# Delta heads of a hybrid decoder: the norm factors of the queries by Newton steps on GpSimd, where a logarithm on ScalarE stood

## The chip, the cores and the metric

The kernel runs on one core of a Trainium2 chip, in one launch. The metric is the device time of that launch in microseconds (us). A time quoted for a kernel is the median of its runs; a profile shows one more execution, which has a time of its own.

The engines are named as in the profile: PE is TensorE (matmuls), PEld its weight loads, DVE is VectorE, ACT is ScalarE, POOL is GpSimd, and SP issues most of the DMAs.

## The reference

Two decoder layers in a row, for 512 prompt tokens and 8 samples of 8 tokens, 576 tokens in all. Each layer has one wide input projection, three branches (a gated linear recurrence, differential attention, gated DeltaNet, 4 heads each), a merge, an output projection, and a gated MLP. Only the DeltaNet branch, the delta heads, matters here:

```python
def l2norm(x):
    return xf * lax.rsqrt(jnp.sum(xf * xf, axis=-1, keepdims=True) + EPS)
...
    q_g = l2norm(cq.reshape(b, L, GD_HEADS, GD_DK)) * (GD_DK ** -0.5)
    k_g = l2norm(ck.reshape(b, L, GD_HEADS, GD_DK))
...
    o_g, gd_s = gdn_chunked(q_g, k_g, v_g, beta, loga, gd_s0)
...
    o_c = (rmsnorm(o_g, w['gdn_norm']) * oz).reshape(b, L, -1).astype(x.dtype)
```

`gdn_chunked` is the gated delta rule, worked block-wise: `o` is linear in the query, and inside a block a unit lower-triangular system with one matrix per block is solved. cq, ck and cv come out of a causal convolution of width 4 and a SiLU.

## The kernel before, in words

**The matmul stream.** Almost all of PE's time goes to the dense projections, in float32 precision. A block of weights `raw` is split into a high part `wh` (a cast on ACT, L264) and a low part `wl` = raw - wh (a subtraction on DVE; `tt`, L197, is the helper that records all two-input tensor operations), and each of the products xh·wh, xl·wh and xh·wl is a matmul into `acc` (recorded at L190, as all matmuls and transposes are). The split parts lie in a pool of three buffers, so that ACT and DVE run about two blocks ahead of PE.

**The order.** `drive` writes the program: dense jobs one after the other, and between their groups of matmuls the steps of stages (a head is a stage) on three lanes. It keeps a model clock that counts the matmuls written so far; a stage says `yield 1.4` where its next matmul wants a result that is to take so long, and is taken up again when the model clock has moved on by that much. On top of it the Tile scheduler orders the instructions of each engine by its own estimate of costs. An engine runs its list strictly in that order.

**A delta head** (`gdn_head`, 4 heads in each of 2 layers) goes through these steps.

- `conv_silu` for the keys, then the sums of squares of the keys, `ss[:, 0]`, and `Ln` of them. From these come the scales `u2` and `w1`.
- `conv_silu` for the queries, and the first weights products (`r<-ckq` on PE).
- The inverse of the triangular matrices in blocks of 16: `cm` goes out by a DMA into `da` and comes back as `dtr` with another layout. A loop of 15 steps, two small DVE operations `dtr<-dtr` each, works out the inverse. It is copied (L858), goes out into `dt` and comes back as `ctt` by DMAs (L860 to L863). Eight DVE operations spread it into `TB`.
- Beside it, `conv_silu` for the values into `cv` (its tanh, `ct`, is L740; its last product on DVE is L742), and the block from L875 on: the queries are transposed and squared on ACT with the sums in `ss[:, 1]` (L880), and `cn`, the factor 1/(norm of the query · sqrt(128)) relative to that of the keys, is worked out of `ss` by a logarithm and an exponential (L881 to L886).
- The larger blocks of the inverse on PE: three rounds, the first of which begins with `r<-TB,ap`. Then the recurrence over four blocks, and the samples' part.
- `finish_gated` at the head's end calls `head_norm` (L491), the only reader of `cn`: it multiplies the mean squares of the output `ot` by `cn` twice, takes `rsqrt` (Newton's steps on DVE, in the kernel already for this), and multiplies the result by `cn`.

Other names in the rows: `XX` is work of the recurrent branch, that the scheduler places beside the delta heads; `thb` (L704) is the SiLU of the output gates; `P<-` on POOL (L1288) clears a tile of attention; `cb<-hg` (L726) copies convolution rows. `L1315` is attention's exponential.

ACT holds one table of functions at a time: a profile row `ACT_TABLE_LOAD` stands wherever the next function needs another one.

Of the kernel before, what the change touches and what calls it, by code (L numbers as in the profile page):

```python
# [11 lines left out]
F32 = mybir.dt.float32  # L12
F32R = mybir.dt.float32r
BF16 = mybir.dt.bfloat16
I32 = mybir.dt.int32
U8 = mybir.dt.uint8
AF = mybir.ActivationFunctionType
ALU = mybir.AluOpType
# [21 lines left out]
EPS = 1e-6  # L40
# [107 lines left out]
def kernel(ctx, tc, a, o, depth=DEPTH, dbg=None):  # L148
    nc = tc.nc
    V, S, G, PE = nc.vector, nc.scalar, nc.gpsimd, nc.tensor  # L150
# [7 lines left out]
    sm = pool('sm', bufs=3)  # L158
# [15 lines left out]
    def bc(ap, n):  # L174
        sh = list(ap.shape)
        return ap.rearrange('p (x o) -> p x o', o=1).to_broadcast([sh[0], sh[1], n])
# [19 lines left out]
    def tt(out, in0, in1, op, eng=None):  # L196
        (eng or V).tensor_tensor(out=out, in0=in0, in1=in1, op=op)  # L197
# [51 lines left out]
    b4e = cst.tile([128, 1], F32, name='b4e')  # L249
# [3 lines left out]
    def rsqrt(out, v, n):  # L253

        y, w = out, sm.tile([128, 20], F32, tag='rs_w', name='rs_w')[:, :n]
        V.tensor_scalar(out=y.bitcast(I32), in0=v.bitcast(I32), scalar1=1, scalar2=None, op0=ALU.logical_shift_right)
        V.tensor_scalar(out=y.bitcast(I32), in0=y.bitcast(I32), scalar1=-1, scalar2=0x5F3759DF, op0=ALU.mult, op1=ALU.add)
        for _ in range(3):
            tt(w, y, y, ALU.mult)
            V.scalar_tensor_tensor(out=w, in0=w, scalar=-0.5, in1=v, op0=ALU.mult, op1=ALU.mult)  # L260
            V.scalar_tensor_tensor(out=y, in0=w, scalar=1.5, in1=y, op0=ALU.add, op1=ALU.mult)

    def split(src, hi, lo):
        S.copy(hi, src)  # L264
        tt(lo, src, hi, ALU.subtract)
# [175 lines left out]
    def norm_stats(sa, rb, r):  # L441

        ps = rp()
        for j in range(5):
            mm(ps[:, j:j + 1], sa[:, 128 * j:128 * j + 128], ones[:, 0:1])
        ms = sm.tile([128, 5], F32, tag='ms', name='ms')
        V.memset(ms, 1.0)
        V.tensor_scalar(out=ms[:, 0:4], in0=ps[:, 0:4], scalar1=1.0 / D_MODEL, scalar2=EPS, op0=ALU.mult, op1=ALU.add)
        V.tensor_scalar(out=ms[:NS, 4:5], in0=ps[:NS, 4:5], scalar1=1.0 / D_MODEL, scalar2=EPS, op0=ALU.mult, op1=ALU.add)
        rsqrt(r, ms, 5)  # L450
        dg = gt.tile([128, T], F32, tag='th', name='dg')
        tt(dg[:, :SEQ].rearrange('p (j t) -> p j t', j=4), bc1(ident, 4), bc(r[:, 0:4], 128), ALU.mult)
        V.tensor_scalar(out=dg[:, SEQ:], in0=ident[:, :NS], scalar1=r[:, 4:5], scalar2=None, op0=ALU.mult)
        yield
        pb, pb2 = rp(), rp()
        mm(pb, ones, dg[:, :SEQ])
        mm(pb2[:, :NS], ones, dg[:, SEQ:])
        S.copy(rb[:, :SEQ], pb)
        S.copy(rb[:, SEQ:], pb2[:, :NS])
# [31 lines left out]
    def head_norm(ot, p, cn=None):  # L491

        sq = p.tile([128, 5, 128], F32, tag='hn', name='hn')
        ms = sm.tile([128, 5], F32, tag='ms', name='ms')
        for j in range(5):
            S.activation(sq[:, j], ot[:, j], AF.Square, accum_out=ms[:, j:j + 1])
        for _ in range(0 if cn is None else 2):
            tt(ms, ms, cn, ALU.mult)
        V.tensor_scalar(out=ms, in0=ms, scalar1=1.0 / 128, scalar2=EPS, op0=ALU.mult, op1=ALU.add)
        r = sm.tile([128, 5], F32, tag='ln_r', name='ln_r')  # L500
        rsqrt(r, ms, 5)
        if cn is not None:
            tt(r, r, cn, ALU.mult)
        tt(ot, ot, bc(r, 128), ALU.mult)
# [133 lines left out]
    for l in range(depth):  # L638
# [82 lines left out]
        def conv_silu(acc, ci, dst):  # L721

            P = cvp.tile([128, 604], F32, tag='cb', name='cb')
            Ps = P[:, 515:603].rearrange('p (b j) -> p b j', j=11)
            G.memset(P[:, 0:3], 0.0)
            G.tensor_copy(Ps[:, :, 0:3], hg[:, ci])  # L726
            tt(P[:, 3:3 + HALF], acc[:, 0], rb[:, 0:HALF], ALU.mult)
            tt(P[:, 3 + HALF:515], acc[:, 1, 0:224], rb[:, HALF:SEQ], ALU.mult)
            tt(Ps[:, :, 3:11], acc[:, 1, 224:288].rearrange('p (b j) -> p b j', j=8),
               rb[:, SEQ:].rearrange('p (b j) -> p b j', j=8), ALU.mult)  # L730
            G.tensor_copy(gco[:, ci, 0, :], P[:, 512:515])
            G.tensor_copy(gco[:, ci, 1:9, :], Ps[:, :, 8:11])
            A = cvp.tile([128, 604], F32, tag='ca', name='ca')
            w = F['gconv']
            S.activation(A[:, 0:600], P[:, 0:600], AF.Copy, scale=w[:, 4 * ci:4 * ci + 1])
            for j in range(1, 4):
                V.scalar_tensor_tensor(out=A[:, 0:600], in0=P[:, j:j + 600], scalar=w[:, 4 * ci + j:4 * ci + j + 1],  # L737
                                       in1=A[:, 0:600], op0=ALU.mult, op1=ALU.add)
            th = gt.tile([128, 604], F32, tag='th', name='ct')
            S.activation(th[:, 0:600], A[:, 0:600], AF.Tanh, scale=0.5)  # L740
            sv = lambda t: t[:, 515:603].rearrange('p (b j) -> p b j', j=11)[:, :, 0:8]
            V.scalar_tensor_tensor(out=dst[:, 0:SEQ], in0=th[:, 0:SEQ], scalar=1.0, in1=A[:, 0:SEQ], op0=ALU.add, op1=ALU.mult)  # L742
            V.scalar_tensor_tensor(out=dst[:, SEQ:].rearrange('p (b j) -> p b j', j=8), in0=sv(th), scalar=1.0, in1=sv(A),
                                   op0=ALU.add, op1=ALU.mult)

        def gdn_head(h, p):
# [15 lines left out]
            ss = sm.tile([128, 2, 5], F32, tag='ss', name='ss')  # L762
# [8 lines left out]
            for j in range(5):  # L771
                n = 128 if j < 4 else NS
# [51 lines left out]

            pc = parts()
            conv_silu(acc, h, ckq[:, 1, 0:T])
            ex = sm.tile([128, 2, 5], F32, tag='ex', name='ex')
            V.tensor_copy(ex[:, 0], u2)
            tt(ex[:, 1], w1, GL[:, :, h], ALU.add)
            S.activation(ex, ex, AF.Exp)  # L830
            nk = sm.tile([128, 5], F32, tag='nk', name='nk')
            V.tensor_scalar(out=nk, in0=ex[:, 0], scalar1=-1.0, scalar2=None, op0=ALU.mult)
# [21 lines left out]
            for s_ in range(15):  # L854
                n, m = 15 - s_, s_ + 1
# [19 lines left out]
            for j in range(5):  # L875
                n = 128 if j < 4 else NS
# [1 line left out]
                trp(pj, ckq[:, 1, 128 * j:128 * j + 128], ident)  # L878
                ks = p.tile([128, 128], F32, tag='U', bufs=2, name='ks')
                S.activation(ks[:n], pj[:n], AF.Square, accum_out=ss[:n, 1, j:j + 1])  # L880
            S.activation(ss[:, 1], ss[:, 1], AF.Ln, bias=b4e)  # L881

            cn = sm.tile([128, 5], F32, tag='cn', name='cn')
            tt(cn, ss[:, 0], ss[:, 1], ALU.subtract)
            V.tensor_scalar(out=cn, in0=cn, scalar1=0.5, scalar2=-0.5 * math.log(128.0), op0=ALU.mult, op1=ALU.add)
            S.activation(cn, cn, AF.Exp)  # L886
            tt(kt[:, 0:4], kt[:, 0:4], bc(ex[:, 1, 0:4], 128), ALU.mult)
            V.tensor_scalar(out=kt[:NS, 4], in0=kt[:NS, 4], scalar1=ex[:NS, 1, 4:5], scalar2=None, op0=ALU.mult)

# [250 lines left out]
        def qk_prep(ti, gi, p):  # L1140
# [15 lines left out]
            V.tensor_scalar(out=ms, in0=ms, scalar1=1.0 / 64, scalar2=EPS, op0=ALU.mult, op1=ALU.add)  # L1156
            r = sm.tile([128, 10], F32, tag='r10', name='r10')
            rsqrt(r, ms, 10)
            rv = r.rearrange('p (j c) -> p j c', c=2)
            tt(rv, rv, bc(rc, 2), ALU.mult)  # L1160
# [214 lines left out]
        for h in range(H):  # L1375
            jobs.append((f'gd{h}', lambda p, h=h: gdn_head(h, p), LR, ('dc',)))
            jobs.append((f'hg{h}', lambda p, h=h: hgrn_head(h, p), LR, ()))
# [90 lines left out]
        for gidx, ng in enumerate(FG):  # L1468
            hid = []
            for i in range(ng):  # L1470
# [18 lines left out]
                w = F['fconv']  # L1489
                S.activation(A[:, 0:592], P[:, 0:592], AF.Copy, scale=w[:, 3 * fi:3 * fi + 1])  # L1490
                for j in range(1, 3):
# [8 lines left out]
                                       op0=ALU.add, op1=ALU.mult)  # L1500
# [150 lines left out]
```

## Time and profile before

| | |
|---|---|
| three runs | 2441.85, 2446.34, 2447.15 us; median 2446.34 |
| profiled execution | 2448.48 us, of which the profile's span is 2446.4 |
| granted TensorE clock, mean of the span | 0.996 |
| busy: PE, DVE, ACT, POOL | 2420.2, 1662.1, 1119.9, 129.0 us |
| table loads on ACT (L881 and L740 among them) | 53, of 1.283 us each |

Busy is the time in which an engine executed an instruction. A row of the timeline gives the start in us, the duration, engine, line, operation, tiles and count, and in brackets how long the engine stood idle before it and for what. A granted clock of 1.0 is 2.4 GHz, 0.5 is 1.2 GHz.

### The profile page before, as it was taken

What the parts mean: (1) busy time and instruction counts of PE and PEld (TensorE: products, weight loads), DVE (VectorE), ACT (ScalarE), POOL (GpSimd) and SP (SyncE); (2) the same over time, 40 slices, a digit from 0 to 9 for tenths busy, and PEclk for the clock granted to TensorE, in tenths of its full rate; (3) what the DMA queues carried; (4) which work ended last, traced back from release to release, by engine and by line L of the source; (5) the groups of instructions that cost most, each with busy time, mean ns of one, the idle gap of its engine ahead of it and who ended that gap; (6) DMA issues with size and microseconds to landing.
All of it is one profiled execution on the core that took longest, in us unless ns stands there. A gap on an engine that the chain in (4) does not pass through costs nothing.

```text
span 2446.4 us, 51847 instructions
## 1 busy us (share of the span) xinstructions
PE 2420.2 (99%) x19602; PEld 2318.1 (95%) x19602; DVE 1662.1 (68%) x4156; ACT 1119.9 (46%) x2401; POOL 129.0 (5%) x444
## 2 busy tenths in 40 slices
PE   9999999999999999999999999999999999999999
PEld 8999988899999999999999998988999999999999
DVE  8787786778765663646677877868676556646464
ACT  6556564646433332323455564646554233323232
POOL 1000000100000010101000010100000000001010
PEclk9999999999999999999999999999999999999999
DMA  6334564554465325252442245564635553242524
GB/s 207 101 99 133 170 204 149 184 175 139 139 204 174 121 83 164 86 161 87 142 137 95 90 163 167 180 213 140 216 103 158 179 177 107 93 153 85 166 83 128
DMA packets 222842, 352.15 MB, mean 144 GB/s; under 512 B 36865, under 2 KB 71809, under 8 KB 222593
## 3 DMA queue, kind: packets, MB, share of 16 engines
q1 hardware_dynamic: 221008, 346.78, 44.4%
q8 instruction: 155, 2.54, 0.4%
q10 hardware_dynamic: 1584, 2.06, 0.3%
q14 instruction: 95, 0.77, 0.1%
HBM read 288.15 MB, written 60.60 MB: 143 GB/s over the span
## 4 chain that ended last, share of the span: by engine, by line
PE 86%; DVE 7%; ACT 3%; DMA 2%; issue 1%; SPq 0%; ACTq 0%; DVEq 0%; POOL 0%
PE acc L190 70%; PE r L190 13%; PE r L194 3%; DVE dtr L197 1%; DVE XX L197 1%; DVE wl L197 1%; DMA ctt<-dt 1%; DMA dtr<-da 1%; DVE ca L737 0%; ACT ks L773 0%; DVE s L528 0%; ACT wh L264 0%; DVE cm L842 0%; DVE ot L197 0%; ACT P L1235 0%
## 5 line engine op out<-in xcount | busy, mean ns | idle before, releaser
L190 PE MATMUL acc<-xh,wh 128*128 128x288 f32 x3584 | 1019.1, 299 | 4.1 <-ACT wh L264 4.1
L190 PE MATMUL acc<-xl,wh 128*128 128x288 f32 x3584 | 1012.8, 298 | 1.1 <-DVE xl L426 1.0
L190 PE MATMUL acc<-xh,wl 128*128 128x288 f32 x3584 | 767.5, 294 | 2.9 <-DVE wl L197 2.8
L264 ACT CAST wh<-raw 128x512 fp32r<-128x512 f32 x624 | 383.1, 614 | 839.4 <-PE acc L190 785.2
L190 PEld LDWEIGHTS acc<-xh,wh 128*128 128x128 f32 x3584 | 675.3, 188 | 20.8 <-issue 13.1
L190 PEld LDWEIGHTS acc<-xl,wh 128*128 128x128 f32 x3584 | 676.8, 189 | 3.8 <-DVE xl L426 2.0
L190 PEld LDWEIGHTS acc<-xh,wl 128*128 128x128 f32 x3584 | 577.8, 188 | 5.7 <-DVE wl L197 4.7
L197 DVE TENSOR_TENSOR wl<-raw,wh 128x512 fp32r<-128x512 f32 x624 | 423.4, 680 | 178.6 <-ACT wh L264 177.7
L190 PE MATMUL acc<-hl,wh 128*128 128x288 f32 x704 | 196.6, 296 | 0.0
L190 PE MATMUL acc<-hh,wh 128*128 128x288 f32 x704 | 194.3, 292 | 0.0
L190 PE MATMUL acc<-hh,wl 128*128 128x288 f32 x704 | 147.1, 290 | 0.0
L190 PEld LDWEIGHTS acc<-hl,wh 128*128 128x128 f32 x704 | 132.3, 188 | 0.0
L190 PEld LDWEIGHTS acc<-hh,wh 128*128 128x128 f32 x704 | 132.0, 188 | 0.0
L190 PEld LDWEIGHTS acc<-hh,wl 128*128 128x128 f32 x704 | 113.1, 188 | 0.0
L190 PE MATMUL acc<-oL,wh 128*128 128x288 f32 x384 | 108.0, 295 | 0.0
L190 PE MATMUL acc<-oh,wh 128*128 128x288 f32 x384 | 107.4, 296 | 0.0
L197 DVE TENSOR_TENSOR cbf<-acc,rb 128x288 f32<-128x288 f32 x132 | 39.1, 351 | 88.9 <-PE acc L190 85.1
L1492 DVE SCALAR_TENSOR_TENSOR caf<-cbf,fm,caf 128x592 f32<-128x592 f32 x88 | 73.5, 835 | 15.1 <-ACT caf L1490 13.5
L190 PE MATMUL acc<-oh,wl 128*128 128x288 f32 x384 | 81.6, 293 | 0.0
L1448 DVE SCALAR_TENSOR_TENSOR xn<-acc,xo 128x576 f32<-128x576 f32 x40 | 30.3, 758 | 70.8 <-PE acc L190 70.8
L190 PEld LDWEIGHTS acc<-oL,wh 128*128 128x128 f32 x384 | 73.0, 190 | 0.0
L190 PEld LDWEIGHTS acc<-oh,wh 128*128 128x128 f32 x384 | 72.1, 188 | 0.1
(425 smaller groups left out, 3626.4 us busy)
## 6 DMA issues: line engine op xcount, KB each, us to landing
raw<-in_w_in_t SPq DMA_DIRECT2D x272, 256.0 KB
raw<-in_w_up SPq DMA_DIRECT2D x176, 256.0 KB
pg<-in_kT SPq DMA_DIRECT2D x128, 256.0 KB
pg<-in_v SPq DMA_DIRECT2D x128, 256.0 KB
raw<-in_w_dn SPq DMA_DIRECT2D x64, 256.0 KB
xo<-xres SPq DMA_DIRECT2D x56, 288.0 KB
thd<-thb SPq DMA_DIRECT2D x48, 288.0 KB
th<-thd SPq DMA_DIRECT2D x48, 288.0 KB
```

The source lines that it names most:

```text
L190: PE.matmul(out, lhsT, rhs, start=start, stop=stop, **kw)
L194: PE.transpose(out, in_, idm)
L197: (eng or V).tensor_tensor(out=out, in0=in0, in1=in1, op=op)
L264: S.copy(hi, src)
L1448: V.scalar_tensor_tensor(out=v2(xn), in0=acc, scalar=0.5, in1=v2(xo), op0=ALU.mult, op1=ALU.add)
L1492: V.scalar_tensor_tensor(out=A[:, 0:592], in0=P[:, j:j + 592], scalar=w[:, 3 * fi + j:3 * fi + j + 1], in1=A[:, 0:592], op0=ALU.mult, op1= ...
```

## The change

In each delta head `cn` is worked out in another way. `Ln` of the queries' sums, the subtraction, the scaling and the `Exp` go. In their place the factor of the keys (half their logarithm, less half the logarithm of 128) becomes a third column block of `ex`, whose exponential is taken anyway (128x10 before, 128x15 now). The reciprocal square root of the queries' sums is started on DVE by an integer shift and a subtraction, and refined by three Newton steps of four small operations each on POOL; a thirteenth POOL operation multiplies by the third block of `ex`. The value of `cn` is the same up to rounding.

```diff
+    def rsqrt_g(out, v, n):
+        y, w = out, sm.tile([128, 20], F32, tag='rs_g', name='rs_g')[:, :n]
+        V.tensor_scalar(out=y.bitcast(I32), in0=v.bitcast(I32), scalar1=1, scalar2=None, op0=ALU.logical_shift_right)
+        V.tensor_scalar(out=y.bitcast(I32), in0=y.bitcast(I32), scalar1=-1, scalar2=0x5F3759DF, op0=ALU.mult, op1=ALU.add)
+        for _ in range(3):
+            tt(w, y, y, ALU.mult, G)
+            tt(w, w, v, ALU.mult, G)
+            G.tensor_scalar(out=w, in0=w, scalar1=-0.5, scalar2=1.5, op0=ALU.mult, op1=ALU.add)
+            tt(y, w, y, ALU.mult, G)
...
-            ex = sm.tile([128, 2, 5], F32, tag='ex', name='ex')
+            ex = sm.tile([128, 3, 5], F32, tag='ex', name='ex')
             V.tensor_copy(ex[:, 0], u2)
             tt(ex[:, 1], w1, GL[:, :, h], ALU.add)
+            V.tensor_scalar(out=ex[:, 2], in0=ss[:, 0], scalar1=0.5, scalar2=-0.5 * math.log(128.0), op0=ALU.mult, op1=ALU.add)
             S.activation(ex, ex, AF.Exp)
...
-            S.activation(ss[:, 1], ss[:, 1], AF.Ln, bias=b4e)
             cn = sm.tile([128, 5], F32, tag='cn', name='cn')
-            tt(cn, ss[:, 0], ss[:, 1], ALU.subtract)
-            V.tensor_scalar(out=cn, in0=cn, scalar1=0.5, scalar2=-0.5 * math.log(128.0), op0=ALU.mult, op1=ALU.add)
-            S.activation(cn, cn, AF.Exp)
+            V.tensor_scalar(out=ss[:, 1], in0=ss[:, 1], scalar1=4 * EPS, scalar2=None, op0=ALU.add)
+            rsqrt_g(cn, ss[:, 1], 5)
+            tt(cn, cn, ex[:, 2], ALU.mult, G)
```

The lists of all engines are ordered anew around the delta heads. Lines of the changed kernel are eleven or twelve higher than those of before. In the whole program the table loads on ACT go from 53 to 37.

On ACT, in the second head of the first layer, the stretch from the squares of the queries (`ks,ss<-r`) to the copies of the values (`bV<-r`) read so before:

```order
L880 ACTIVATE ks,ss<-r 128x128 x2
L880 ACTIVATE ks,ss<-r 64x128
L881 ACT_TABLE_LOAD
L881 ACTIVATE ss<-ss,b4e 128x5
L264 CAST wh<-raw 128x512
L1020 COPY XX<-acc 128x576
L740 ACT_TABLE_LOAD
L740 ACTIVATE ct<-ca 128x600
L886 ACTIVATE cn<-cn 128x5
L264 CAST wh<-raw 128x512
L905 ACTIVATE bV<-r 128x512
```

and it reads so now:

```order
L892 ACTIVATE ks,ss<-r 128x128 x2
L892 ACTIVATE ks,ss<-r 64x128
L275 CAST wh<-raw 128x512
L1031 COPY XX<-acc 128x576
L751 ACTIVATE ct<-ca 128x600
L275 CAST wh<-raw 128x512
L916 ACTIVATE bV<-r 128x512
```

The logarithm, the exponential and both table loads are gone, and the rest keeps its order.

On DVE, in the fourth head of a layer, the end of the 15 steps (`dtr<-dtr`) and the copy behind them stood so before:

```order
L1054 COPY_PREDICATED ATs<-cu,r 64x16x2
L197 TENSOR_TENSOR dtr<-dtr 36x2x14
L704 SCALAR_TENSOR_TENSOR thb<-acc,rb 128x576
L197 TENSOR_TENSOR dtr<-dtr 36x15
L197 TENSOR_TENSOR XX<-G 128x32x8
L197 TENSOR_TENSOR dtr<-dtr 36x15
L197 TENSOR_TENSOR XX<-G 128x32x8
L858 COPY dtr<-dtr 36x256
L197 TENSOR_TENSOR wl<-raw,wh 128x512
L197 TENSOR_TENSOR XX<-XX,k 128x32x8
L197 TENSOR_TENSOR XX<-XX,q 128x32x8
```

and they stand so now:

```order
L197 TENSOR_TENSOR XX<-G 128x32x8
L197 TENSOR_TENSOR dtr<-dtr 36x2x14
L197 TENSOR_TENSOR wl<-raw,wh 128x512
L197 TENSOR_TENSOR dtr<-dtr 36x2x14
L197 TENSOR_TENSOR XX<-XX,k 128x32x8
L197 TENSOR_TENSOR dtr<-dtr 36x15
L197 TENSOR_TENSOR XX<-XX,q 128x32x8
L197 TENSOR_TENSOR dtr<-dtr 36x15
L197 TENSOR_TENSOR wl<-raw,wh 128x512
L870 COPY dtr<-dtr 36x256
L715 SCALAR_TENSOR_TENSOR thb<-acc,rb 128x576
```

Ahead of the copy there are now two `wl` and two `XX` more than before. In the second and third head there are two `XX` and one `thb` more, in the first none.

On PE the matmuls are the same, and places shift by up to some twenty. Between a head's weights products and its first `r<-TB,ap` stood 157, 151, 151 and 177 dense matmuls in heads one to four of either layer; now it is 151, 155, 165 and 187 in the first layer and 157, 155, 165 and 187 in the second.

On POOL, in the first head, what stood between the clearing of `ot` and the clearing of `P` was nothing; now there is the chain, with an instruction without a tile ahead of it, which the compiler sets once in the program:

```order
L945 MEMSET ot 64x128
L197 ISA
L197 TENSOR_TENSOR rs_g<-cn 128x5
L197 TENSOR_TENSOR rs_g<-rs_g,ss 128x5
L271 TENSOR_SCALAR rs_g<-rs_g 128x5
L197 TENSOR_TENSOR cn<-rs_g,cn 128x5
...
L197 TENSOR_TENSOR cn<-cn,ex 128x5
L1299 MEMSET P 128x64
L986 MEMSET Rs 64x128
```

The clearings of `P` and `Rs` are now queued behind thirteen operations.

## Rows read from the trace of the kernel before

**Rows 1.** The page: busy time of each engine, share of the span, instructions.

```profile
PE 2420.2 (99%) x19602; PEld 2318.1 (95%) x19602; DVE 1662.1 (68%) x4156; ACT 1119.9 (46%) x2401; POOL 129.0 (5%) x444
```

**Rows 2.** What PE waited for: us in total, times, longest.

```profile
PE r L190 <- DVE TB L197: 4.2, 4, 1.9
PE acc L190 <- ACT wh L264: 4.1, 3, 2.0
PE acc L190 <- DVE wl L197: 2.8, 5, 1.3
```

**Rows 3.** Timeline of PE: a dense stretch; then stalls and first reads of TB.

```profile
260.22 0.29 PE L190 MATMUL acc<-xh,wh 128*128 128x288 f32 x1
...
261.93 0.29 PE L190 MATMUL acc<-xl,wh 128*128 128x288 f32 x1
...
274.52 0.41 PE L190 MATMUL r<-TB,ap 128*128 128x64 f32 x2 [0.21 <-DVE TB L197]
387.94 0.43 PE L190 MATMUL r<-TB,ap 128*128 128x64 f32 x2 [1.21 <-DVE TB L197]
464.70 0.40 PE L190 MATMUL acc<-xh,wh 128*128 128x288 f32 x1 [1.95 <-ACT wh L264]
619.30 0.43 PE L190 MATMUL r<-TB,ap 128*128 128x64 f32 x2
1597.05 0.43 PE L190 MATMUL r<-TB,ap 128*128 128x64 f32 x2 [0.83 <-DVE TB L197]
1670.77 0.40 PE L190 MATMUL acc<-xh,wh 128*128 128x288 f32 x1 [1.95 <-ACT wh L264]
1825.17 0.43 PE L190 MATMUL r<-TB,ap 128*128 128x64 f32 x2 [1.95 <-DVE TB L197]
```

**Rows 4.** Windows behind stalls: length, PE busy, granted clock, DMA share, GB/s.

```profile
389.95:396.80 6.85, 6.85 (x33) 0.50 0.91 317
464.98:468.46 3.48, 3.48 (x16) 0.51 0.22 75
1826.96:1833.80 6.84, 6.84 (x33) 0.50 0.15 53
```

**Rows 5.** ACT's groups by line: count | busy us, mean ns | idle before.

```profile
L740 ACT ACT_TABLE_LOAD x14 | 18.0, 1283 | 0.2
L881 ACT ACT_TABLE_LOAD x8 | 10.3, 1283 | 0.1
L881 ACT ACTIVATE ss<-ss,b4e 128x5 f32<-128x5 f32 x8 | 2.4, 299 | 0.1
L886 ACT ACTIVATE cn<-cn 128x5 f32<-128x5 f32 x8 | 1.5, 191 | 0.0
```

**Rows 6.** Timeline of DVE, heads one and two: products that waited for the tanh.

```profile
254.51 0.69 DVE L742 SCALAR_TENSOR_TENSOR cv<-ct,ca 128x512 f32<-128x512 f32 x1 [0.51 <-ACT ct L740]
368.42 0.69 DVE L742 SCALAR_TENSOR_TENSOR cv<-ct,ca 128x512 f32<-128x512 f32 x1 [0.29 <-ACT ct L740]
```

**Rows 7.** Timeline of DVE, fourth head of layer one: from the steps to TB.

```profile
600.79 0.60 DVE L197 TENSOR_TENSOR dtr<-dtr 36x15 f32<-36x15 f32 x3 [0.47 <-DMA dtr<-da]
...
612.77 0.37 DVE L858 COPY dtr<-dtr 36x256 f32<-36x256 f32 x1
613.07 0.67 DVE L197 TENSOR_TENSOR wl<-raw,wh 128x512 fp32r<-128x512 f32 x1
613.67 0.41 DVE L197 TENSOR_TENSOR XX<-XX,k 128x256 f32<-128x256 f32 x1
614.00 0.41 DVE L197 TENSOR_TENSOR XX<-XX,q 128x256 f32<-128x256 f32 x1
614.34 0.74 DVE L704 SCALAR_TENSOR_TENSOR thb<-acc,rb 128x576 f32<-128x576 f32 x1
615.00 0.67 DVE L197 TENSOR_TENSOR wl<-raw,wh 128x512 fp32r<-128x512 f32 x1
...
618.96 1.71 DVE L197 TENSOR_TENSOR TB<-ctt,cf 128x128 f32<-128x128 f32 x8 [0.72 <-DMA ctt<-dt]
```

**Rows 8.** POOL's small operations, and DVE beside one of them.

```profile
252.67 1.31 POOL L726 COPY cb<-hg 128x24 f32<-128x24 f32 x1
253.20 0.69 DVE L197 TENSOR_TENSOR wl<-raw,wh 128x512 fp32r<-128x512 f32 x1
L197 DVE TENSOR_TENSOR wl<-raw,wh x624: 549/685/736, 6.6 to 2435.0; 128x512 fp32r<-128x512 f32 x156
L726 POOL COPY cb<-hg x24: 205/282/1308, 17.9 to 1765.8; 128x24 f32<-128x24 f32 x24
291.15 0.15 POOL L1288 MEMSET P<- 128x64 f32 x1 [36.91 <-PE r L194]
```

**Rows 9.** Tile cn and its readers: min/median/max ns, first and last start.

```profile
L886 ACT ACTIVATE cn<-cn x8: 190/191/192, 254.4 to 1803.6; 128x5 f32<-128x5 f32 x8
L197 DVE TENSOR_TENSOR ms<-ms,cn x16: 153/166/168, 314.1 to 1864.9; 128x5 f32<-128x5 f32 x16
L885 DVE TENSOR_SCALAR cn<-cn x8: 157/166/196, 253.8 to 1801.4; 128x5 f32<-128x5 f32 x8
```

## The prediction

> **What bounds the kernel now.** The page's first part comes first: PE is busy for 2420.2 us, 99% of the span of 2446.4, DVE for 68%, ACT for 46%, POOL for 5% [rows 1]. So PE is the bound almost everywhere, and only two things can change the time: the 26 us in which PE stands idle (2446.4 - 2420.2), and PE's clock, since a matmul at half clock counts as busy and takes twice as long.
>
> The list of waits comes next, to see which idle time lies near the change. DVE's TB holds PE four times for 4.2 us in all, ACT's wh three times for 4.1, DVE's wl five times for 2.8 [rows 2]. The timeline places them: four of the eight delta heads reach their first `r<-TB,ap` too early, by 0.21, 1.21, 0.83 and 1.95 us, and twice, once in each layer, wh is late by 1.95 us [rows 3]. The fourth head of the first layer, at 619.30, has no wait.
>
> Windows behind these stalls show the third thing: after the stalls at 387.94, 464.70 and 1825.17 the granted clock is about 0.5, that is 1.2 GHz, for 6.85, 3.48 and 6.84 us, with PE busy all along [rows 4]. Such a window does half the work, so it costs half its length: 3.4, 1.7 and 3.4 us, more than the stalls themselves. The fourth stall over 1.2 us, at 1670.77, has no such window behind it, nor have those of 0.83 and 0.21 us. Three falls in four for long stalls, none for the short ones: a stall near 1.2 us decides over 3.4 us.
>
> **ACT's part of the change.** Eight times the logarithm with its table load goes (10.3 + 2.4 us) and eight exponentials (1.5) [rows 5]. The tanh behind them then finds its table in place: eight of the L740 loads go too, at 1.283 us each, 10.3 [rows 5]. Together 24.5 us. None of it is on the path by itself: ACT is busy 46% of the time, wh is cast up to two blocks ahead, and the two long waits for wh at 464.70 and 1670.77 lie where attention's exponential stands, whose order on ACT is unchanged. What ACT gives directly is small: near the first head the tanh comes earlier, so that DVE's cv no longer waits 0.51 us, in the second 0.29 [rows 6].
>
> **DVE's part.** Two small instructions go and four come, two more per head at some 0.166 us [rows 9], 2.7 us of busy time in all. At most 0.33 us of it stands in the chain of a head; I count nothing for it, because the order of DVE moves by more than that, as follows. If the cover is gone it costs 0.33 us in each head that waits for TB.
>
> **The order around TB** is what carries the sum. The chain runs from the 15 steps through the copy (L858), two DMAs and the eight operations of TB to PE; in the fourth head it takes from 600.79 to 619.30, and what DVE does inside it ahead of the copy delays all that follows [rows 3, 7]. By the new order the heads get more work there: heads two and three one thb and two XX, 0.66 + 0.67 = 1.33 us by the pitch of starts; the fourth head two wl and two XX, 2 × 0.60 + 0.67 = 1.87 us [rows 7]. PE, for its part, comes to its first read later when more dense matmuls stand ahead. They follow each other at 0.131 us, thirteen in 261.93 - 260.22 [rows 3].
>
> The wait after the change is the wait before, plus DVE's lateness, less 0.131 us per dense matmul added.
> - First heads: layer one has six matmuls fewer, 0.79 us, and cv's 0.51 us gone: the wait of 0.21 becomes 0.49 (+0.28). Layer two: no matmul moved, no wait in the rows, nothing.
> - Second heads: 1.33 - 0.29 of cv [rows 6] - 4 × 0.131 = +0.52. The waits go from 1.21 to 1.73 and from 0.83 to 1.35.
> - Third heads: 1.33 - 14 × 0.131 = -0.50 where no wait stood: nothing.
> - Fourth heads: 1.87 - 10 × 0.131 = +0.56: at most 0 to 0.56 in layer one, and 1.95 to 2.51 in layer two.
>
> Sum of the waits: 0.28 + 2 × 0.52 + 2 × 0.56 = +2.4 us. The bounds are 0, if what was added is taken in gaps that DVE has, and 0.28 + 2 × 1.04 + 2 × 1.87 = 6.1, if only DVE's lateness counts and PE's later arrival gives nothing. I take 2.4.
>
> **The clock.** The wait in layer two's second head passes from 0.83, behind which the clock held, to 1.35, above the 1.21 behind which it fell [rows 3, 4]. With waits that long followed by a fall in most cases but not in all, I take half of 3.4: +1.7. The two falls that are there stay. Bounds: 0 and 3.4.
>
> **POOL's part.** No row has a small arithmetic operation on POOL. The nearest are a clearing of 0.15 us and the small copies, 0.205 at least, 0.282 in the median, 1.308 at most [rows 8]. Thirteen of them make 2.7 to 17 us per head; I take the median, 3.7 us. The instruction without a tile, once in the program, is bounded by nothing and by the longest copy, 1.3 us. Both are hidden: cn was there at 254.4 and first read at 314.1, 60 us later, also in the last head (1803.6 and 1864.9) [rows 9], and the clearing of P that is now queued behind the chain came after 36.91 us of idle POOL [rows 8]. So 0.
>
> The Trainium skill, GPSIMD Engine Reference, section Instruction dispatch, gives some 6 us for the first call of a freshly loaded POOL kernel; no row here shows one. As an estimate, by that page the sum would be the same, since one such delay fits into the same 60 us.
>
> **Sum**: +2.4 + 1.7 = +4.1 on the profiled execution's own 2448.5, so 2452.6. That execution was 2.1 us over the median of the runs; against that median the same sum gives 2450.5, or +0.17%. A measurement here can tell about 0.2% from no change: the three runs of before alone span 2441.9 to 2447.2.
>
> **Rivals.**
>
> *Faster: the TB waits and their clock falls go.* ACT has 24.5 us less, and wh, thb and the XX copies come earlier; if DVE therefore does its extra work in gaps where it now waits (0.47 us before the steps, 0.72 before TB [rows 7], and cv's), the chain ends earlier than now. All four waits gone are 4.2 us, the two falls behind them 6.8: 2446.3 - 11.0 = 2435.3. With only one fall avoided, 3.4 + 1.2, it is 2441.7. Against it: the inserted operations stand in the chain by the list that DVE must follow, and the wait before TB is for a DMA whose start that chain sets. 0.20, with 0.18 faster by over 0.2%.
>
> *Nothing shows: the 24.5 us lay beside PE, and the moved rows fall into slack.* For it: 46% of ACT, and waits of 11 us in all for DVE and ACT [rows 1, 2]. The time is 2446.3, give or take 3. 0.16.
>
> *Slower: POOL's chain holds DVE.* The new chain is released by the queries' sums, just when the 15 steps run on DVE, which are two-input operations on the same memory. If each POOL operation held DVE for its length, 13 × 0.205 = 2.7 us would come on top in each head [rows 8]. In the five heads with a wait or none to spare that is 13.3 us, and the waits of the three that kept their clock (274.52, 619.30, 1597.05 [rows 3]) would pass 1.2 us: 3 × 3.4, of which 1.7 is counted above. 2446.3 + 4.1 + 13.3 + 8.5 = 2472. It decides from a hold of about 0.1 us per operation (1.3 us a head) on. Against it: where a POOL copy lay beside wl on DVE, the copy took 1.31 us instead of 0.28 and wl 0.69, which is its median of 0.685: POOL waited, and DVE did not [rows 8]. 0.12.
>
> The Trainium skill, SBUF — State Buffer, section Who interferes with whom, says that a DVE instruction with two inputs in SBUF and a GpSimd instruction that reads SBUF share a port, and that whoever starts first blocks the other fully. By that rule both outcomes are possible; the copy beside wl shows one order of them, and an operation on POOL that starts first is shown by no row here.
>
> *Slower: the clock behind wh.* The stalls at 464.70 and 1670.77 recur, and the second one kept its clock [rows 3, 4]. A fall there costs 1.7 to 3.4 on top of the sum: about 2453 to 2455. 0.07.
>
> **How the numbers follow.** The forecast, a small loss, has 0.45 and 2447.5 to 2454, with 2450.5 as its middle; two fifths of it lie above 2451.2, the bound of slower by 0.2%: 0.18 slower, 0.27 same. With the rivals: faster 0.18; same 0.27 + 0.16 + 0.02 = 0.45; slower 0.18 + 0.12 + 0.07 = 0.37. For the range, 2441 leaves about 0.12 of the faster cases below, and 2461 about 0.08 of POOL's case above.
>
> **What would show it.** Table loads on ACT 37 in place of 53, ACT busy near 1095 us, PE within 8 us of 2420. Waits for TB near 6.5 us in all, with 1.3 to 1.8 in both second heads and 2.5 in the last head; the half clock behind them, once more than before if the step on the clock is right. The wait of 1.95 for wh twice again. POOL's chain done long before the mean squares' first product with cn, its operations at 0.2 to 0.3 us, and dtr, wl and TB on DVE at their old durations. The forecast is wrong if the TB waits shrink (then the first rival), if dtr or wl take longer beside the chain (the third), or if a fall of the clock comes or goes at a place that has nothing to do with a delta head.

## The result, and the profile after

The changed kernel takes 2463.64 us (median of 4 runs, 2461.38 to 2466.09), the kernel before 2446.5 (median of 4). The ratio is 1.0078, with a 95% interval of 1.0066 to 1.009: slower by 16 to 22 us, and outside the range that was forecast. The profiled execution took 2466.09, its span 2464.3.

The page, busy time of each engine, against [rows 1]:

```profile
PE 2432.0 (99%) x19602; PEld 2329.6 (95%) x19602; DVE 1659.8 (67%) x4172; ACT 1098.7 (45%) x2369; POOL 160.4 (7%) x548
```

ACT has 21 us less, as meant. The span is 17.9 us longer, and PE accounts for 11.8 of it as *busy* time, with the same 19602 matmuls. Only 6.1 us are idle time. So most of the loss is not a wait.

The first suspect is the clock. The windows at half clock in this execution, apart from the last microseconds:

```profile
466.05:469.46 3.41, 3.41 (x16) 0.50 0.36 96
1725.57:1732.40 6.83, 6.83 (x32) 0.50 0.16 49
```

That is 10.2 us, against 17.2 in [rows 4]. In such a window a dense matmul starts every 240 ns, against 131 at full clock, as three starts of before show:

```profile
393.29 0.44 PE L190 MATMUL acc<-xl,wh 128*128 128x288 f32 x1
393.53 0.44 PE L190 MATMUL acc<-xh,wh 128*128 128x288 f32 x1
393.77 0.44 PE L190 MATMUL acc<-xl,wh 128*128 128x288 f32 x1
```

So a window costs about 45% of its length, and of the 6.9 us of difference some 3 were *gained*. The clock is not what made PE busy for longer: the matmuls are slower at full clock.

To find where, each matmul's start was set against that of the same place in the list of before. Up to 650 us the two traces stay within 4 us of each other. Between 680 and 1245 us, where both programs run merge and MLP in the same order, without a delta head, the lag grows from 0.6 to 8.2 us; in layer two's MLP, from 1,930 us on, by another 7.6. Two windows of 39 us there, the first almost all down-projection (`acc<-hh`, `acc<-hl`, the high and low part of the hidden layer), the second up-projection (`acc<-xh`, `acc<-xl`), in the kernel before:

```profile
1060.00:1099.00 39.00, 39.00 (x302) 1.00 0.63 200
1110.00:1149.00 39.00, 39.00 (x303) 1.00 0.28 88
```

and in the changed kernel, at the same clock:

```profile
1060.00:1099.00 39.00, 39.00 (x295) 1.00 0.58 184
1110.00:1149.00 39.00, 39.00 (x298) 1.00 0.27 82
```

The count in brackets is that of the matmuls; two or three of it reach over an edge. Over both layers, starts in the down-projection stand 130.0 ns apart before and 133.3 after; in the up-projection 130.05 and 131.7; in the output projection ahead of the MLP (`mh`, `ml`) 131.7 and 133.3. With 2,110, 4,210 and 770 of them that is 7.0 + 6.9 + 1.3 = 15.2 us, which is the lag of 7.6 us that each layer adds.

The waits of PE, against [rows 2]:

```profile
PE r L190 <- DVE dtr L197: 5.6, 6, 1.4
PE r L190 <- DVE TB L197: 5.0, 6, 1.4
PE acc L190 <- ACT wh L275: 4.1, 2, 2.1
PE acc L190 <- DVE wl L197: 3.5, 5, 1.3
```

The sum for TB moved a little, 4.2 to 5.0. New is most of the first line: six waits of `r<-XX`, products of the recurrent branch, before which DVE's last signal is one from the 15 steps. Before there were two of them:

```profile
PE r L190 <- DVE dtr L197: 0.5, 2, 0.3
```

The timeline, of the first head's chain, of the second head, and of the first head of layer two, shows where they come from:

```profile
253.22 0.20 POOL L945 MEMSET ot<- 64x128 f32 x1
253.51 0.25 POOL L197 TENSOR_TENSOR rs_g<-cn 128x5 f32<-128x5 f32 x1
253.83 0.52 POOL L197 TENSOR_TENSOR rs_g<-rs_g,ss 128x5 f32<-128x5 f32 x1
254.45 0.65 POOL L271 TENSOR_SCALAR rs_g<-rs_g 128x5 f32<-128x5 f32 x1
...
368.18 0.19 POOL L197 TENSOR_TENSOR rs_g<-cn 128x5 f32<-128x5 f32 x1
...
370.69 0.20 POOL L197 TENSOR_TENSOR rs_g<-rs_g,ss 128x5 f32<-128x5 f32 x1
370.95 0.07 DVE L774 MEMSET ss<- 128x10 f32 x1 [2.80 <-POOL rs_g L197]
371.00 0.41 DVE L197 TENSOR_TENSOR dtr<-dtr 36x15 f32<-36x15 f32 x2
371.55 0.53 POOL L197 TENSOR_TENSOR cn<-cn,ex 128x5 f32<-128x5 f32 x1
372.85 1.30 PE L190 MATMUL r<-XX 128*128 128x128 f32 x10 [1.40 <-DVE dtr L197]
379.25 1.27 PE L190 MATMUL r<-XX 128*128 128x64 f32 x10 [1.12 <-DVE dtr L197]
391.05 0.43 PE L190 MATMUL r<-TB,ap 128*128 128x64 f32 x2 [1.39 <-DVE TB L197]
...
621.79 0.66 PE L190 MATMUL r<-TB,ap 128*128 128x64 f32 x4 [1.02 <-DVE TB L197]
...
1475.14 0.20 POOL L197 TENSOR_TENSOR rs_g<-rs_g,ss 128x5 f32<-128x5 f32 x1
1475.39 0.16 DVE L197 TENSOR_TENSOR dtr<-dtr 36x15 f32<-36x15 f32 x1 [2.06 <-issue]
1475.40 0.07 DVE L774 MEMSET ss<- 128x10 f32 x1
1476.73 1.30 PE L190 MATMUL r<-XX 128*128 128x128 f32 x10 [0.89 <-DVE dtr L197]
1483.38 1.27 PE L190 MATMUL r<-XX 128*128 128x64 f32 x10 [0.94 <-DVE dtr L197]
...
1723.48 0.66 PE L190 MATMUL r<-TB,ap 128*128 128x64 f32 x4 [1.04 <-DVE TB L197]
```

`ss` has three buffers. DVE clears the one for the head three later, and the scheduler puts that clearing right where the buffer should come free. Before, the buffer's last reader was DVE itself. Now it is the chain's last multiplication by `ss`, at 370.69: DVE stands for 2.80 us, with the 15 steps and the XX work queued behind a clearing that is needed only three heads later, in the next layer. The third head has the same stall, of 2.40 us; DVE's waits name both:

```profile
DVE ss L774 <- POOL rs_g L197: 5.2, 2, 2.8
```

Two more stalls look the same and stand in the profile under other names, because the clearing and the step behind it start within 0.02 us of each other: 1.87 us in the fourth head (put down to a DMA) and 2.06 us in layer two's first (put down to nothing, the row at 1475.39). Both end 0.05 to 0.07 us after the chain's last multiplication by `ss`, as the other two do. That makes 9.1 us of DVE in four heads, and the six waits of `r<-XX` lie in these four.

### The profile page after: what moved, and what is told of

The parts are those of the page before. It is cut to its first block, busy times and chain, and to the rows that moved or that the text cites. A ratio compares the mean times of both kernels' runs of the same rounds, so it can differ in the third digit from the quotient of the medians.

```text
span 2464.3 us, 51952 instructions
## 1 busy us (share of the span) xinstructions
PE 2432.0 (99%) x19602; PEld 2329.6 (95%) x19602; DVE 1659.8 (67%) x4172; ACT 1098.7 (45%) x2369; POOL 160.4 (7%) x548
## 3 DMA queue, kind: packets, MB, share of 16 engines
q10 hardware_dynamic: 1584, 2.06, 0.3%
## 4 chain that ended last, share of the span: by engine, by line
PE 86%; DVE 8%; DMA 2%; ACT 2%; issue 2%; SPq 0%; DVEq 0%; ACTq 0%
PE acc L190 70%; PE r L190 13%; PE r L194 3%; DVE wl L197 1%; DVE dtr L197 1%; DMA ctt<-dt 1%; DVE XX L197 1%; DMA dt<-dtr 1%; DMA pg<-in_v 0%; DVE s L539 0%; DVE ca L748 0%; SPq L1292 0%; DVE ot L197 0%; ACT P L1246 0%; DMA dtr<-da 0%
```

## The experiments

Two things had changed that the diff does not speak of. The scratch tile `rs_g`, three buffers of 96 bytes, lies in the small-tile pool, and the tiles allocated behind that pool lie 288 bytes higher: in the built program `hh` begins at byte 123936 of a partition of SBUF, the on-chip memory, in place of 123648, which is 32 past a multiple of 256 instead of on one. The tiles `xh`, `xl`, `wh` and `wl` lie where they were. And GpSimd now reads `ss`.

**Theory 1**: the placement slows the matmuls, some 13 to 15 us. **Theory 2**, the rival: the new order, or work in the heads, sets another pace. **Theory 3**, the prediction's own rival: GpSimd's chain holds DVE.

### Formula against placement

`before_shift288`, and with `[128, 64]` in its place `before_shift768`: the old formula, tiles moved.

```diff
-            cn = sm.tile([128, 5], F32, tag='cn', name='cn')
+            cn = sm.tile([128, 5], F32, tag='cn', name='cn'); sm.tile([128, 20], F32, tag='rs_g', name='rs_g')
```

`after_same_place`: the new formula, tiles where they were; `after_shift768` has a tile of `[128, 64]` there instead.

```diff
-        y, w = out, sm.tile([128, 20], F32, tag='rs_g', name='rs_g')[:, :n]
+        y, w = out, sm.tile([128, 20], F32, tag='rs_w', name='rs_g')[:, :n]
```

> The kernel before, with the scratch tile of the change (three buffers of 96 bytes) reserved but never used: the same instructions in the same order, and every tile that lies behind it in SBUF 288 bytes higher, as in the kernel after. Theory 1 (placement decides the pace of the dense matmuls): the matmuls after the delta heads run at 131.7 to 133.3 ns as in the kernel after, and the time is about 2446 + 14 = 2460 us. Theory 2 (the order or the work in the heads decides it): 130.0 ns there as before, 2446 us within 0.2%.

> The kernel after, with the scratch of the Newton steps on GpSimd taken out of the tiles that the other Newton routine has already: the same order on every engine as after, and all other tiles where they lay before. Theory 1 (placement): the pace of 130.0 ns comes back, and what is left is the moved order's: about 2463.6 - 14 = 2450 us. Theory 2 (order or work): 2463 us as after. Theory 3 (GpSimd's chain holds DVE, and that costs the most): 2463 us as well, with long operations on DVE beside the chain.

> The kernel before with a larger unused tile: 3 times 256 bytes, so every tile behind it keeps its place modulo 256 bytes. Theory 1a (the place modulo 64 bytes decides the pace): 2446 us as before. Theory 1b (any shift changes it, by a rhythm that is caught or missed): anywhere from 2443 to 2462, with stretches at 130.0, 131.7 and 133.3 ns. Theory 2: 2446 us.

> The kernel after with a scratch tile of 256 bytes in place of 96, so that all tiles behind it are 768 bytes higher than before, a multiple of 256. Theory 1a: as with the scratch in its old place, about 2450 us. Theory 1b: between 2447 and 2466. Theory 2 and 3: 2463 us.

| tiles behind the pool, bytes higher | old formula | new formula |
|---|---|---|
| 0 | 2445.54 | 2449.14, ratio 1.0016 (1.0007 to 1.0025) |
| 288 | 2458.61, ratio 1.0047 (1.0034 to 1.006) | 2463.64 beside 2446.5, ratio 1.0078 (above) |
| 768 | 2446.02, ratio 0.9998 (0.9989 to 1.0007) | 2449.57, ratio 1.0018 (1.0009 to 1.0027) |

The old formula with 288 unused bytes, its instructions in the old order, has the slow matmuls of the changed kernel:

```profile
1060.00:1099.00 39.00, 39.00 (x295) 1.00 0.57 183
1110.00:1149.00 39.00, 39.00 (x298) 1.00 0.26 87
```

and the new formula at the old place (`after_same_place`) has the quick ones:

```profile
1060.00:1099.00 39.00, 39.00 (x302) 1.00 0.62 199
1110.00:1149.00 39.00, 39.00 (x303) 1.00 0.27 89
```

The ratios are to the kernel before, run beside each. Theory 1 holds, theory 2 falls, and theory 3 does not make the main loss: by the medians 13 us go with the placement in the old formula and some 14 in the new, and some 4 with the formula in either good placement. 768 bytes, which keep the place modulo 256, cost nothing.

### Which places are quick

Four more kernels have the instructions and order of before and only tiles elsewhere: unused small tiles of `[128, 16]` (`before_shift192`) and `[128, 8]` (`before_shift96`), or a reserve at the upper end of SBUF, which moves the right-hand stack with `oh` and `oL`, the merge's operands; 96 bytes of it are `before_right96`, and `[128, 56]` together with an unused small tile of `[128, 32]` is `before_both384`. For `before_right32`:

```diff
-    xst = stage('x', 'right')
+    padr = ctx.enter_context(stage('padr', 'right')); padr.tile([128, 8], F32, name='padr'); xst = stage('x', 'right')
```

> The kernel before with an unused tile of 3 times 64 bytes, so every tile behind it is 192 bytes higher: a multiple of 64, not of 128 or 256. Same instructions and order. If the place modulo 64 bytes decides the pace: 2446 us as before, the hidden layer's matmuls (hh, hl) at 130.0 ns. If modulo 128 or 256: about 2458, with 133.3 ns there.

Measured: 2457.97, ratio 1.0063 (1.005 to 1.0076). A multiple of 64 is not enough.

> The kernel before with 32 bytes reserved at the upper end of SBUF, so that the tiles of the right-hand stack, oh and oL of the merge among them, begin at multiples of 64 bytes instead of 32 past one. Same instructions and order. By the placement theory the matmuls that read oh and oL go from 132.3 to 130.0 ns (1150 of them, 2.6 us), those on mh and ml after them from 131.7 to 130.0 (768, 1.3 us): about 2442 us. If only the left-hand tiles matter: 2446 us.

Measured: 2447.62, ratio 1.0011 (1.0001 to 1.002); `oh` and `oL` became slower, 134.4 ns, where the expectation had them quicker.

> The kernel before with 96 bytes reserved at the upper end of SBUF: oh and oL begin at multiples of 128 bytes (128 past one of 256). Same instructions and order. So far a tile's pace went with its place modulo 256: 0 gave 130.0 ns, 32 gave 133.3, 192 gave 134.4, 224 gave 132.2. A matmul reads one half of a tile, and the halves are 1152 bytes apart, 128 modulo 256, so places 128 apart should be alike. If so: oh and oL at 130.0 to 131.7 ns, mh and ml after them at 130.0, 1.3 to 4 us less than before: 2441 to 2444 us. If only 0 modulo 256 is quick: oh and oL at 132 to 135 ns and 2445 to 2449 us.

Measured: 2445.45, ratio 1.0002 (0.999 to 1.0014); `oh` and `oL` at 132.5 ns in the mean. That mean is of two paces, 131.7 in layer one and 133.3 in layer two. So the guess that places 128 apart are alike came out in one layer and missed in the other.

> The kernel before with an unused tile of 3 times 32 bytes: hh, hl, mh and ml at 96 past a multiple of 256. Same instructions and order. If places 128 apart are alike, 96 goes with 224: the hidden layer's matmuls at 132.2 ns, 2111 of them in the profile, 4.7 us, and with mh, ml and the projections between them 6 to 12 us over before: 2451 to 2457 us. If they are not alike, 133 to 135 ns and 2455 to 2460.

Measured: 2456.81, ratio 1.0058 (1.0044 to 1.0072); `hh` at 133.3 ns, not the 132.2 of that guess.

> The kernel before with 384 unused bytes below the left-hand tiles and 224 at the upper end: hh, hl, mh and ml lie 128 past a multiple of 256, oh and oL at a multiple. Same instructions and order. It swaps the two places that the runs so far could not tell apart. If 128 is as good as 0: hh and hl at 130.0 ns, and the time within 0.2% of before. If only 0 is good: hh and hl at 132 ns or more, some 5 us and more over before. Separately, oh and oL: at 130.0 to 131.7 ns if a multiple of 256 is what they lacked, at 132.2 or more if something else holds them.

Measured: 2455.66, ratio 1.0047 (1.0033 to 1.0062); `hh` at 132.7, `oh` at 131.7 ns. The first is again of two paces: 131.7 in each layer's first stretch of down-projection, 133.3 in the two behind it.

Together, the mean distance of starts at full clock and without a wait, by the tile's first byte modulo 256:

| place | hh, hl (2,110) | oh, oL (1,150) |
|---|---|---|
| 0 | 130.0 | 131.7 |
| 32 | 133.3 | |
| 96 | 133.3 | |
| 128 | 132.7 (131.7 and 133.3) | 132.5 (131.7 and 133.3) |
| 192 | 134.3 | 134.4 |
| 224 | | 132.3 (before) |

Of the places tried only a multiple of 256 gives 130.0 to `hh`; `oh` is best there too, but does not reach it. The first byte modulo 256 sorts these runs; that it is the mechanism is not shown. A matmul reads one half of a tile, and the halves begin 1152 bytes apart, which is 128 modulo 256. So with the tile at 0 or at 128 the matmuls start at the same two places, and still `hh` runs at 130.0 in the one case and at 131.7 or 133.3 in the other. The windows of `before_shift192`, with the same two stretches, show the worst place:

```profile
1060.00:1099.00 39.00, 39.00 (x293) 1.00 0.59 191
1110.00:1149.00 39.00, 39.00 (x298) 1.00 0.27 86
```

The up-projection's operands never moved, and yet its window has 298 in place of 303 whenever `hh` lies badly. The stretch of up-projection ahead of the first down-projection is different: it slowed to 131.7 with the tiles at 32, and stayed at 130.1 with them at 96, 128 and 192. That was not taken apart.

The Trainium skill, SBUF — State Buffer, section Operand start alignment, asks of an operand's start only that it be a multiple of its element's size, and says that this is about what is legal, not about speed. All places here are legal by it; the runs add a price of up to 3%.

### The formula's own 4 us

`after_own_sum` is `after_shift768` with the chain's operand in the scratch tile, so that GpSimd does not read `ss`; `own_sum_right32` and `own_sum_right96` add the reserves at the upper end. Against the changed kernel:

```diff
-        y, w = out, sm.tile([128, 20], F32, tag='rs_g', name='rs_g')[:, :n]
+        y, w = out, gs[:, :n]
...
-            V.tensor_scalar(out=ss[:, 1], in0=ss[:, 1], scalar1=4 * EPS, scalar2=None, op0=ALU.add)
-            rsqrt_g(cn, ss[:, 1], 5)
+            gs = sm.tile([128, 64], F32, tag='rs_g', name='rs_g')
+            V.tensor_scalar(out=gs[:, 32:37], in0=ss[:, 1], scalar1=4 * EPS, scalar2=None, op0=ALU.add)
+            rsqrt_g(cn, gs[:, 32:37], 5, gs)
```

> The kernel after with a 256-byte scratch tile (the placement that costs nothing), and the queries' sums written into that tile too, so that GpSimd no longer reads ss and the clearing of ss for the head three later no longer waits for GpSimd's chain. Theory A (DVE's two stalls of 2.8 and 2.4 us at that clearing make the waits of PE for XX and TB in heads two and three): those waits shrink by 3 to 5 us, and the time is about 2445 us. Theory B (the moved order makes them): they stay, 2449 to 2450 us.

Measured: 2448.29, ratio 1.0017 (1.0007 to 1.0026), no gain that shows, so theory A's time did not come. But the waits did go, as it said. PE's list with `ss` read by the chain (`after_shift768`):

```profile
PE r L190 <- DVE dtr L197: 5.6, 6, 1.4
PE r L190 <- DVE TB L197: 4.8, 5, 1.5
```

and without (`after_own_sum`), where the first of them is gone:

```profile
PE r L190 <- DVE TB L197: 6.2, 6, 2.2
PE acc L190 <- ACT wh L275: 4.0, 2, 2.0
```

What came in their place are windows at half clock. Of `after_own_sum`:

```profile
463.72:467.14 3.42, 3.42 (x17) 0.50 0.28 87
620.74:627.56 6.82, 6.82 (x33) 0.50 0.34 118
1675.46:1678.87 3.41, 3.41 (x15) 0.50 0.27 77
1719.83:1726.66 6.83, 6.83 (x32) 0.50 0.20 66
```

These are 20.5 us, and at 45% cost some 9. The profile of `after_shift768` has one such window before the end, 6.8 us, which cost some 3. So in these two executions 5.6 us of waits for XX went, 1.4 us more of waits for TB came, and some 6 us of slow matmuls. That the one brought the other is not shown by one execution of each.

The results give a mean clock for each run, and so the two can be told apart over all runs. At a mean clock of 0.999, and on the same chip, before takes 2442.4 (median of 5) and `after_shift768` 2448.4 (of 7): 6 us more. `after_own_sum` had no run at 0.999: its 11 runs lie at 0.996 to 0.998, those of `after_shift768` at 0.997 to 0.999. At 0.997 `after_own_sum` takes 2448.0 (7 runs), and before on its chip 2447.7 (5). So at equal clock most of the 6 us is gone once GpSimd is off `ss`; `own_sum_right96` below says the same, with 1.0 us. These are few runs, and a thousandth of the mean clock is some 2 us. What `after_own_sum` loses is a lower clock, 0.997 in the median against 0.998 for before beside it. Why its clock is lower stays open.

> Both of the last two edits on the kernel after: placement mended on both sides, and GpSimd's chain off the buffer that DVE clears. If placement and the wait add up: about 2441 us, below the kernel before. If the moved order is what costs: about 2445 us.

Measured: 2448.73, ratio 1.0018 (1.0007 to 1.0028), with `oh` at 134.4 ns, so neither of the two expectations came out.

> The kernel after with its scratch at the place that costs nothing, GpSimd's chain off the buffer that DVE clears, and 96 bytes reserved at the upper end. It is own_sum_right32 with another reserve: if places modulo 128 decide, oh and oL go from 134.4 to 130.0 or 131.7 ns, and the time from 2448.7 to 2444 us or so; else no change beyond 0.1%.

Measured: 2443.67, ratio 1.0004 (0.9995 to 1.0013), beside 2443.78 for before. At a mean clock of 0.999 it takes 2442.3 (5 runs), and before 2441.3 (6 runs). The time is the one that was expected, but not for its reason: `oh` runs at 132.4 ns, where the kernel before has 132.3. What differs from `after_own_sum` is the clock, 0.998 in the median against 0.997. This is the new formula at its best here: equal to the kernel before, not quicker. No version beat before.

## Why the prediction was wrong

**The step that failed by most is the first: "only two things can change the time"**, PE's idle time and PE's clock. It put the cost of a matmul at full clock at no change, without a reason. That cost changed: 130.0 to 133.3 ns in the down-projection and 130.05 to 131.7 in the up-projection, 15.2 us in the traces. The diff's new tile `rs_g` alone, unused, costs 13 us (`before_shift288`). That is three quarters of the loss. At equal placement the change costs 0.16 to 0.18%, 3.6 to 4.0 us by the medians; the forecast was 4.1. The sum was right by accident, as its parts show.

**POOL's part: "So 0".** The chain was sized well: 3.7 us forecast, and in the second head, from 368.18 to 372.08, it is 3.9. It is also true that `cn` is read long after and that P's clearing waits for nothing. The step asked who waits for what the chain *writes* and for what is queued behind it, and not who waits for the buffer that it *reads*. That was DVE, in four heads for 1.87 to 2.80 us, and it made PE's waits for XX, 5.6 us where before had 0.5. `after_own_sum` shows this: with the operand elsewhere those waits are gone.

**The order around TB.** Forecast 6.6 us of waits in all; 5.0 in the profile after, 6.2 without DVE's stalls. The sum is near and its parts are not. In heads one to four the forecast was 0.49, 1.73, 0 and at most 0.56 in layer one, and 0, 1.35, 0 and 2.51 in layer two. The profile after has 0, 1.39, 0 and 1.02, and 0.31, 0.88, 1.04 and 0.40. The last head, which was to wait longest, waits 0.40, and the third head of layer two, where the matmuls added were to cover everything, waits 1.04. Two of the parts held roughly (1.39, and 0.88 where 0.83 stood before); adding DVE's lateness and PE's later arrival head by head did not give the rest, and why was not taken apart.

**The clock: +1.7.** Here the sign was wrong: windows at half clock fell from 17.2 to 10.2 us. The stall of 1.39 us at 391.05 kept its clock, where 1.21 at 387.94 had lost it [rows 3, 4], with stalls of 1.40 and 1.12 us ahead of it besides; the one fall behind TB came after the 1.04 us at 1723.48. That a stall near 1.2 us decides did not hold. The price per window was a little high too: a dense matmul at half clock took 240 ns against 131, 1.8 times and not twice, so by that price 6.84 us cost 3.1 and not 3.4. One profile is no basis for such a term: before itself, in 23 runs on one chip, ran at mean clocks from 0.994 to 1.000, from 2453.0 to 2439.0 us.

**ACT's part** came out as said: 21.2 us less busy time, forecast 24.5, and nothing of it on the path. The two waits for wh of 2 us are still there.

**The rivals.** That POOL's chain holds DVE operation by operation is refuted; it held DVE by the buffer, as said. The subtraction wl took 685 ns in the median and 736 at most [rows 8], and takes 684 and 725 after; the 15 steps, 201 and 223 before, took 200 and 257:

```profile
L197 DVE TENSOR_TENSOR wl<-raw,wh x624: 551/684/725, 6.0 to 2452.7; 128x512 fp32r<-128x512 f32 x156
L197 DVE TENSOR_TENSOR dtr<-dtr x240: 154/200/257, 255.0 to 1832.7; 36x15 f32<-36x15 f32 x16, 36x28 f32<-36x28 f32 x16, 36x39 f32<-36x39 f32 x16, 36x48 f32<-36x48 f32 x16
L197 POOL TENSOR_TENSOR rs_g<-rs_g,ss x24: 197/198/700, 253.8 to 1820.8; 128x5 f32<-128x5 f32 x24
```

The chain's operations take 0.20 us where DVE is idle, and up to 0.70 beside DVE: GpSimd waited. The order that the prediction had no row for, POOL first, occurs too: a step that began inside a POOL operation took at most 0.04 us longer than the longest of its shape before. The first operation on POOL came 0.09 us after the clearing ahead of it had ended (253.22 + 0.20, 253.51); the 6 us that the Trainium skill gives for a first call (GPSIMD Engine Reference, Instruction dispatch) do not show here. The first rival, that TB's waits go, did not happen in the sum. The rival "slower" had the right sign by a mechanism that did not act.

## What to carry to other kernels

A new tile, however small, moves all that is allocated behind it: where matmuls bound a kernel, compare the first bytes of their moving operands modulo 256 before and after, and test a change of formula with the tiles held in place. When work moves to a slow queue, ask who waits for the buffers that it reads, a clearing for a much later use included; the scheduler places such a clearing by its own estimate of when the buffer comes free. Take a term on the clock from many runs, not from one trace, and compare two kernels at equal mean clock: the waits that were removed here show as a gain only so.

## What the runs showed of the hardware that was not expected

The matmul stream has a rhythm that repeats to the nanosecond: in the down-projection six starts in 780 ns (130.0 each) before and twelve in 1600 (133.3) after, in the up-projection twelve in 1580 (131.7) after, with the same instructions. Which of them holds depends on where the moving operand lies, but not on that alone: `mh` at a multiple of 256 ran at 131.7, and the up-projection at 130.05 or 131.7 without being moved. What ties a stretch to the one ahead of it stays open, and so does why the place counts.

Within one kernel, runs differ by their mean clock: on one chip before took 2440.9 to 2444.6 us at 0.998, 2440.2 to 2442.9 at 0.999 and 2439.0 at 1.000. That is the spread of its runs, and it is as large as the formula's own 4 us.
